# Gate and up products of the gated feed-forward parts by Strassen's scheme, in halves of 11 blocks

## The chip, the core and the metric

The kernel runs on one NeuronCore of a Trainium2 chip. Five engines work side by side, each through its own instruction queue in order: TensorE (PE, matrix products into PSUM), VectorE (DVE), ScalarE (ACT), GpSimd (POOL) and SyncE (SP, which issues DMAs). The metric is the device time of one execution in microseconds, as the median of several runs.

## What is computed

The reference is two transformer-like blocks over 512 tokens of width 1024. The first has two layers, each with a gated feed-forward part, a mixer of three kinds of heads, and a second gated feed-forward part. The second has a gated linear attention layer and a sparse attention layer, each followed by a convolutional feed-forward part. The change touches the four gated parts alone:

```python
def _swiglu(x, w_gate, w_up, w_down):
    return (jax.nn.silu(x @ w_gate) * (x @ w_up)) @ w_down

for l in range(DEPTH):                      # DEPTH = 2, D_FF = 2816
    x = x + 0.5 * _swiglu(_rms_norm(x, norm_ffn1[l]), ffn1_w_gate[l], ffn1_w_up[l], ffn1_w_down[l])
    ...                                     # mixer
    x = x + 0.5 * _swiglu(_rms_norm(x, norm_ffn2[l]), ffn2_w_gate[l], ffn2_w_up[l], ffn2_w_down[l])
```

All inputs are float32.

## The kernel before, in words

Activations lie feature-major: `x` is eight tiles of 128 features by 512 tokens. A float32 product is made of three reduced-precision (`float32r`) products: each operand is cut into a high part (ACT copies it into a `float32r` tile) and a low part (DVE subtracts the high part from the original), and PE accumulates hi x hi, hi x lo and lo x hi. `load_w` (L252) does this for a weight piece: a DMA on SP's queue into `raw`, ACT into `whi` (L258), DVE into `wlo` (L259). `raw` has three buffers, `whi` and `wlo` two each. `gemm` (L262) then issues three matmuls for each block of 128 inputs (L270 to L272), all with 512 tokens as columns.

A gated part is `ffn` (L361). `scaled` (L339) multiplies each `x` tile by the norm's gain and cuts it into `xh` and `xl`. `norm_r` (L321) computes the tokens' inverse norm R beside it: ACT squares, POOL adds the squares (L331), PE sums over partitions, and R comes as a tile `bR`. Then 22 blocks of 128 hidden features follow. Each has a gate product and an up product, of eight input blocks and three matmuls each (48 matmuls). DVE multiplies the gate product by R out of PSUM (L371), ACT applies silu (L372), POOL multiplies by R again (L373), DVE multiplies by the up product out of PSUM (L374), and `split` cuts the hidden block `h` (L287, L288). Afterwards `down` (L353) makes eight rows of output, each over all 22 hidden blocks in three weight pieces (66 matmuls), and DVE adds each to `x` (L359).

PSUM banks rotate through six names, so three blocks can be in flight. The order of instructions on each engine is set by a scheduler, from the order in which the code is written, priorities and a timeline of its own; buffers and semaphores hold whatever comes too early. The two convolutional parts (`conv_ffn`) have the same products and another elementwise chain; the change leaves their code as it is.

## Time and profile before

| | us |
|---|---|
| median of 3 runs | 3472.16 (3469.72 to 3480.32) |
| profiled execution, its own time | 3467.64 |
| its span, first to last instruction | 3464.6 |
| PE busy | 3419.1 (99%) |
| DVE busy | 1748.7 (50%) |
| ACT busy | 1232.1 (36%) |
| POOL busy | 538.8 (16%) |
| mean granted PE clock | 0.996 |

The span is what the trace covers; the profiled execution's own time has 3.0 us more around it. A row of the trace names the line of the kernel, the engine, the operation and the tiles (out<-in), and gives durations; an interval of idle time before an instruction stands in brackets with what ended it. The end of a matmul is modelled, and matmuls overlap: what one costs in a stream is the distance between two starts.

### The profile page before, as it was taken

The numbers are of one execution on the slowest core, as the hardware profiler recorded it, in microseconds if no ns is written. First come the engines' busy times: TensorE is split into PE (matmuls) and PEld (weight loads), VectorE is DVE, ScalarE is ACT, GpSimd is POOL, SyncE is SP. The second block draws the span as 40 slices with busy tenths as digits, with TensorE's granted clock in tenths as the row PEclk, the third lists the DMA queues.
The fourth block names the chain that finished last, engine by engine and source line by source line (L and its number), as shares of the span: only waits on it lengthen the run. The fifth ranks groups of instructions, "written<-read, shape, count | busy, mean of one in ns | idle before, by whom it ended". The sixth has DMA issues, their size and how long they took to land.

```text
span 3464.6 us, 43276 instructions
## 1 busy us (share of the span) xinstructions
PE 3419.1 (99%) x17126; PEld 2729.0 (79%) x17126; DVE 1748.7 (50%) x2857; ACT 1232.1 (36%) x1946; POOL 538.8 (16%) x509
## 2 busy tenths in 40 slices
PE   8999999999999999999999999999999999999998
PEld 6888777878888888877778888777888887778886
DVE  5333498663333433359765333385655354465532
ACT  3222334442222322233444222343433244643332
POOL 2110025011111111012401110020211000211100
PEclk9999999999999999999999999999999999999999
DMA  4223322132233223322123223322322333132232
GB/s 138 94 92 109 101 85 64 40 126 95 94 91 98 91 97 93 109 94 78 54 96 106 94 95 103 110 68 70 107 92 96 106 121 97 49 98 94 97 91 80
DMA packets 127593, 321.55 MB, mean 93 GB/s; under 512 B 32384, under 2 KB 34976, under 8 KB 127392
## 3 DMA queue, kind: packets, MB, share of 16 engines
q1 hardware_dynamic: 127392, 318.80, 29.0%
q8 instruction: 134, 2.20, 0.3%
q14 instruction: 67, 0.55, 0.0%
HBM read 303.81 MB, written 14.94 MB: 92 GB/s over the span
## 4 chain that ended last, share of the span: by engine, by line
PE 94%; DVE 3%; POOL 1%; DMA 1%; issue 1%; ACT 0%; SPq 0%; DVEq 0%; POOLq 0%; ACTq 0%
PE mm L272 13%; PE mm L270 13%; PE mm L271 13%; PE at L271 8%; PE at L270 8%; PE at L272 8%; PE rr L272 4%; PE rr L271 4%; PE rr L270 4%; PE rx L272 3%; PE rx L270 3%; PE rx L271 3%; PE po L749 1%; PE at L799 1%; PE at L743 1%
## 5 line engine op out<-in xcount | busy, mean ns | idle before, releaser
L258 ACT ACTIVATE whi<-raw 128x1024 fp32r<-128x1024 f32 (+2 forms) x566 | 562.6, 995 | 1685.2 <-issue 528.8
L259 DVE TENSOR_TENSOR wlo<-raw,whi 128x1024 fp32r<-128x1024 f32 (+2 forms) x566 | 650.7, 1150 | 502.0 <-ACT whi L258 486.2
L270 PE MATMUL mm<-xh,whi 128*128 128x512 f32 x1216 | 485.1, 399 | 9.1 <-ACT whi L258 9.0
L272 PE MATMUL mm<-xh,wlo 128*128 128x512 f32 x1216 | 487.5, 401 | 0.0
L271 PE MATMUL mm<-xl,whi 128*128 128x512 f32 x1216 | 484.7, 399 | 0.8 <-DVE xl L347 0.7
L272 PE MATMUL at<-xh,wlo 128*128 128x512 f32 x736 | 291.3, 396 | 0.0
L270 PE MATMUL at<-xh,whi 128*128 128x512 f32 x736 | 291.1, 395 | 0.0
L271 PE MATMUL at<-xl,whi 128*128 128x512 f32 x736 | 291.0, 395 | 0.0
L373 POOL TENSOR_TENSOR fg<-fg,bR 128x512 f32<-128x512 f32 x88 | 155.2, 1765 | 806.6 <-ACT fg L372 806.6
L270 PEld LDWEIGHTS mm<-xh,whi 128*128 128x128 f32 x1216 | 228.9, 188 | 65.1 <-ACT whi L258 9.5
L272 PEld LDWEIGHTS mm<-xh,wlo 128*128 128x128 f32 x1216 | 228.7, 188 | 60.6 <-issue 3.9
L271 PEld LDWEIGHTS mm<-xl,whi 128*128 128x128 f32 x1216 | 228.7, 188 | 57.3 <-issue 2.5
L270 PE MATMUL mm<-hi,whi 128*128 128x512 f32 x652 | 259.8, 400 | 3.3 <-ACT hi L287 1.5
L271 PE MATMUL mm<-lo,whi 128*128 128x512 f32 x652 | 258.2, 396 | 0.1
L272 PE MATMUL mm<-hi,wlo 128*128 128x512 f32 x652 | 257.5, 396 | 0.0
L331 POOL TENSOR_TENSOR nacc<-nacc,nsq 128x512 f32<-128x512 f32 x70 | 107.0, 1529 | 781.3 <-ACT nsq L330 780.8
L272 PEld LDWEIGHTS at<-xh,wlo 128*128 128x128 f32 x736 | 138.1, 188 | 35.5 <-DVE wl L514 1.5
L271 PEld LDWEIGHTS at<-xl,whi 128*128 128x128 f32 x736 | 138.2, 188 | 34.8 <-issue 1.5
L272 PE MATMUL rr<-xh,wlo 128*128 128x512 f32 x416 | 164.8, 396 | 0.8 <-DVE wlo L259 0.8
L270 PEld LDWEIGHTS at<-xh,whi 128*128 128x128 f32 x736 | 138.2, 188 | 34.1 <-ACT gy L1005 0.8
L271 PE MATMUL rr<-xl,whi 128*128 128x512 f32 x416 | 164.3, 395 | 0.0
L270 PE MATMUL rr<-xh,whi 128*128 128x512 f32 x416 | 164.2, 395 | 0.0
(667 smaller groups left out, 5878.8 us busy)
## 6 DMA issues: line engine op xcount, KB each, us to landing
raw<-ffn_gu SPq DMA_DIRECT2D x176, 512.0 KB
raw<-c_gu SPq DMA_DIRECT2D x88, 512.0 KB
raw<-ffn_dn SPq DMA_DIRECT2D x64, 448.0 KB
raw<-w_in SPq DMA_DIRECT2D x46, 512.0 KB
raw<-ffn_dn SPq DMA_DIRECT2D x32, 512.0 KB
raw<-c_dn SPq DMA_DIRECT2D x32, 448.0 KB
raw<-a_w_in SPq DMA_DIRECT2D x17, 512.0 KB
park<-x SPq DMA_DIRECT2D x32, 256.0 KB
```

Source lines behind the costliest of these rows:

```text
L258: self.A.activation(hi, raw, AF.Copy)
L259: self.V.tensor_tensor(lo, raw, hi.bitcast(F32), OP.subtract)
L270: self.T.matmul(ps, wh, xh, start=first and j == 0, stop=False)
L271: self.T.matmul(ps, wh, xl, start=False, stop=False)
L272: self.T.matmul(ps, wl, xh, start=False, stop=last and j == nk - 1)
L331: self.G.tensor_tensor(acc, acc, sq, OP.add)
L373: self.G.tensor_tensor(g, g, R, OP.mult)
L743: self.T.transpose(pt[:, b * 128:(b + 1) * 128], P[h][:, b * 128:(b + 1) * 128], self.ident)
L749: self.T.matmul(po[64 * h:64 * h + 64, i * 128:(i + 1) * 128], V(h, b), PT[h][:, b * 128:(b + 1) * 128], start=b == 0, stop=b == i)
L799: self.T.matmul(ps, q[b, i * 128:(i + 1) * 128], k[b, 0:(i + 1) * 128], start=True, stop=True)
```

## The change

For each block of 128 hidden features, gate and up together are a product of a 2 x 1024 block of weights with 1024 x 512 activations. The change splits the inputs into two halves of 512 features (p and q) and the tokens into two halves of 256 (a and b), and so has the 2 x 2 by 2 x 2 form on which Strassen's scheme (in Winograd's form) needs seven products in place of eight. Each product is over four blocks of 128 inputs, with three matmuls each and 256 columns.

`seven_x` takes the place of `scaled`. It forms the seven combinations of activations once for a part, and cuts each into hi and lo. `gate_up` takes the place of the two `proj` calls: POOL forms three sums and differences of the raw weight halves (s1, s2, and two written back into `ru` and `rg`), the weights are cut as G, S, U (each a `whi`/`wlo` pair of 1024 elements) and W (512), PE makes products 1 to 7 into two PSUM banks X and Y, and ACT and DVE combine them into gate and up. R for the up product moves from the block's chain into the addition of the output. The 22 blocks are worked in two halves of 11, each followed by a down product over its 11 hidden blocks (two weight pieces a row) that is added to `x`, on POOL after the first half and on DVE after the second. `raw` gets four buffers and `whi`/`wlo` three. At the start of the kernel two raw weight pieces are loaded early in place of two cut ones.

```diff
+HALF = ["r1"] * 8 + ["aq"] * 3
...
+    def raw(self, dram, cols):
+        raw = self.wp.tile([128, cols], F32, tag="raw", name=self.nm("raw"), bufs=4)
+        self.S.dma_start(raw, dram)
+        return raw
+
+    def parts(self, cols):
+        return [self.wp.tile([128, cols], F32R, tag=tag, name=self.nm(tag), bufs=3) for tag in ("whi", "wlo")]
...
+    def cut(self, src, hi, lo):
+        self.A.activation(hi, src, AF.Copy)
+        self.V.tensor_tensor(lo, src, hi.bitcast(F32), OP.subtract)
+
+    def seven_x(self, x, gname, l0):
...
+        for j in range(4):
+            scale(j)
+            self.V.tensor_tensor(xg[j][:, b], xg[j][:, b], xg[j][:, a], OP.subtract)
+            hi, lo = pair(self.other)
+            self.cut(xg[j], hi, lo)
...
+        for j in range(4):
+            scale(4 + j)
...
+            self.V.tensor_tensor(c[:, a], y[:, b], xg[j][:, b], OP.subtract)
+            self.V.tensor_tensor(c[:, b], y[:, a], c[:, a], OP.subtract)
+            hi, lo = pair(self.home)
+            self.cut(c, hi, lo)
...
+            self.cut(y, hi, lo)
...
+            self.V.tensor_tensor(d[:, e], c[:, a], xg[j][:, a], OP.subtract)
+            self.cut(d[:, e], dh[:, e], dl[:, e])
...
+    def gate_up(self, wgu, f, F, R):
...
+        s1, s2 = [self.s([128, H], "ws", heap="r0") for _ in range(2)]
+        S, G, U = self.parts(D), self.parts(D), self.parts(D)
+        self.G.tensor_tensor(s1, ru[:, p], ru[:, q], OP.add)
+        self.G.tensor_tensor(s2, s1, rg[:, p], OP.subtract)
+        self.cut(rg, *G)
+        self.cut(s2, *[t[:, q] for t in S])
+        self.cut(s1, *[t[:, p] for t in S])
+        self.G.tensor_tensor(ru[:, p], rg[:, p], ru[:, p], OP.subtract)
+        self.cut(ru, *U)
+        self.G.tensor_tensor(rg[:, q], rg[:, q], s2, OP.subtract)
...
+        self.cut(rg[:, q], *W)
...
+        A = {1: half(G, p), 2: half(G, q), 3: W, 4: half(U, q), 5: half(S, p), 6: half(S, q), 7: half(U, p)}
...
+                self.T.matmul(ps, hi[:, w], xh, start=first and j == 0, stop=False, skip_group_check=True)
+                self.T.matmul(ps, hi[:, w], xl, start=False, stop=False, skip_group_check=True)
+                self.T.matmul(ps, lo[:, w], xh, start=False, stop=j == 3, skip_group_check=True)
...
+        product(1, X[:, a], True)
+        self.A.activation(P[:, a], X[:, a], AF.Copy)
...
+                product(6, B, True)
+                self.V.tensor_tensor(v[:, a], B, P[:, a], OP.add)
...
+                product(5, X[:, b])
+                self.A.activation(P[:, b], X[:, b], AF.Copy)
+        product(4, E)
+        product(2, X[:, a])
+        self.V.tensor_tensor(g[:, a], X[:, a], R[:, a], OP.mult)
+        product(7, B)
+        self.V.tensor_tensor(v[:, b], B, P[:, a], OP.add)
+        self.V.tensor_tensor(u[:, a], E, v[:, b], OP.add)
+        self.V.tensor_tensor(u[:, b], v[:, b], P[:, b], OP.add)
+        product(3, X[:, b])
+        self.V.tensor_tensor(g[:, b], X[:, b], v[:, a], OP.add)
+        self.G.tensor_tensor(g[:, b], g[:, b], R[:, b], OP.mult)
+        self.A.activation(g, g, AF.Silu)
+        self.V.tensor_tensor(g, u, g, OP.mult)
+        return g
...
     def ffn(self, x, l, nm, wgu, wdn):
         self.on("o", "rr")
-        xs = self.scaled(x, nm, KT * l)
+        F = self.seven_x(x, nm, KT * l)
         R = self.norm_r(x)
...
-        for f in range(NF):
...
-        self.down(x, h.__getitem__, wdn, 0.5)
+        for part in range(2):
+            h = [self.split(self.gate_up(wgu, part * NF // 2 + i, F, R), None, HALF[i]) for i in range(NF // 2)]
+            for n in range(KT):
+                pd = self.ps([128, T], next(self.banks))
+                for a, b in ((0, 6), (6, 11)):
+                    o = part * NF // 2
+                    w = self.load_w(wdn[n, :, (o + a) * 128:(o + b) * 128], (b - a) * 128)
+                    self.gemm(pd, w, h.__getitem__, a, b, a == 0, b == NF // 2)
+                y = self.s([128, T], "fd")
+                self.V.scalar_tensor_tensor(y, pd, 0.5, R, OP.mult, OP.mult)
+                (self.V if part else self.G).tensor_tensor(x[n], x[n], y, OP.add)
```

In the words of the prediction, v_a and v_b, u_a and u_b, g_a and g_b are the halves of the tiles `fv`, `fu` and `fg` over tokens a and b; h hi and h lo are the cut hidden block.

On DVE, in the middle of a gate and up stage, this stands in the queue before, for one block and the start of the next (`lo` is the hidden block, `fg` the gate):

```order
L288 TENSOR_TENSOR lo_105_615<-fg_103_609,hi_104_614 128x512
L371 TENSOR_TENSOR fg_114_680<-mm_109_624,bR_45_202 128x512
L259 TENSOR_TENSOR wlo_119_692<-raw_117_689,whi_118_691 128x1024
L374 TENSOR_TENSOR fg_114_680<-rr_113_655,fg_114_680 128x512
L259 TENSOR_TENSOR wlo_123_723<-raw_121_720,whi_122_722 128x1024
L288 TENSOR_TENSOR lo_116_686<-fg_114_680,hi_115_685 128x512
```

and this after, at the same place in the first part, from the low part of the next block's G to that block's U:

```order
L373 TENSOR_TENSOR wlo_497_3053<-raw_490_3044,whi_496_3052 128x1024
L463 TENSOR_TENSOR fg_485_2942<-mm_482_2939,bR_67_260 128x256
L472 TENSOR_TENSOR fg_465_2809<-fu_466_2810,fg_465_2809 128x512
L465 TENSOR_TENSOR fv_487_2944<-rr_483_2940,wp_484_2941 128x256
L297 TENSOR_TENSOR lo_469_2908<-fg_465_2809,hi_468_2907 128x512
L466 TENSOR_TENSOR fu_486_2943<-rr_483_2940,fv_487_2944 128x256
L467 TENSOR_TENSOR fu_486_2943<-fv_487_2944,wp_484_2941 128x256
L373 TENSOR_TENSOR wlo_495_3051<-ws_492_3048,whi_494_3050 128x512
L469 TENSOR_TENSOR fg_485_2942<-mm_482_2939,fv_487_2944 128x256
L373 TENSOR_TENSOR wlo_495_3051<-ws_493_3049,whi_494_3050 128x512
L373 TENSOR_TENSOR wlo_499_3055<-raw_491_3046,whi_498_3054 128x1024
```

Between two blocks' G stand now thirteen operations (the eleven shown, and two more: v_a and W), where five stood for a block; the G of the next block comes before the last products of this one.

On POOL, behind the seven additions of squares at the start of the first part, this stands before:

```order
L331 TENSOR_TENSOR nacc_31_152<-nacc_31_152,nsq_37_169 128x512
L331 TENSOR_TENSOR nacc_31_152<-nacc_31_152,nsq_38_172 128x512
L373 TENSOR_TENSOR fg_48_254<-fg_48_254,bR_45_202 128x512
L373 TENSOR_TENSOR fg_59_325<-fg_59_325,bR_45_202 128x512
```

and this after (`ws` are s1 and s2 of block 0, `raw` its weights):

```order
L340 TENSOR_TENSOR nacc_53_210<-nacc_53_210,nsq_59_227 128x512
L340 TENSOR_TENSOR nacc_53_210<-nacc_53_210,nsq_60_230 128x512
L427 TENSOR_TENSOR ws_68_262<-raw_10_89 128x512
L428 TENSOR_TENSOR ws_69_263<-ws_68_262,raw_9_84 128x512
L432 TENSOR_TENSOR raw_10_89<-raw_9_84,raw_10_89 128x512
L434 TENSOR_TENSOR raw_9_84<-raw_9_84,ws_69_263 128x512
```

Where POOL went from the norm to one multiplication a block, it now forms block 0's weights behind the norm, and later repeats four such operations and one multiplication of 256 elements for every block:

```order
L427 TENSOR_TENSOR ws_492_3048<-raw_491_3046 128x512
L428 TENSOR_TENSOR ws_493_3049<-ws_492_3048,raw_490_3044 128x512
L432 TENSOR_TENSOR raw_491_3046<-raw_490_3044,raw_491_3046 128x512
L434 TENSOR_TENSOR raw_490_3044<-raw_490_3044,ws_493_3049 128x512
L470 TENSOR_TENSOR fg_485_2942<-fg_485_2942,bR_67_260 128x256
```

## Rows read from the trace of the kernel before

**Rows 1.** The page: span, and busy time of each engine.
```profile
span 3464.6 us, 43276 instructions
PE 3419.1 (99%) x17126; PEld 2729.0 (79%) x17126; DVE 1748.7 (50%) x2857; ACT 1232.1 (36%) x1946; POOL 538.8 (16%) x509
```
**Rows 2.** Busy time by stretch: 18 gate/up blocks, the kernel's start, one PE wait.
```profile
core 0: us, PE busy (x) PEld busy (x) DVE busy (x) ACT busy (x) POOL busy (x), PEclk, DMA share, GB/s
48.70:250.30 201.60, 201.60 (x866) 162.18 (x865) 79.83 (x90) 57.60 (x73) 32.60 (x18) 1.00 0.29 95
9.00:48.70 39.70, 38.02 (x158) 28.94 (x159) 26.53 (x34) 19.48 (x28) 16.52 (x10) 1.00 0.42 149
2394.00:2402.00 8.00, 6.43 (x20) 4.52 (x19) 3.65 (x6) 2.27 (x4) 0.00 (x0) 0.79 0.31 97
```
**Rows 3.** Timeline (start us, duration us) of DVE: two outputs of a down product.
```profile
276.86 0.69 DVE L359 SCALAR_TENSOR_TENSOR x<-at,x 128x512 f32<-128x512 f32 x1 [2.82 <-PE at L272]
292.26 0.69 DVE L359 SCALAR_TENSOR_TENSOR x<-mm,x 128x512 f32<-128x512 f32 x1 [2.82 <-PE mm L272]
```
**Rows 4.** Timeline of PE: first and last of 23 matmuls of 256 columns.
```profile
1795.33 0.28 PE L271 MATMUL mm<-ml,whi 128*128 128x256 f32 x1
...
1797.97 0.28 PE L272 MATMUL mm<-mh,wlo 128*128 128x256 f32 x1
```
**Rows 5.** Groups of DVE, same 18 blocks: count, then busy us, mean ns, idle before.
```profile
L259 DVE TENSOR_TENSOR wlo<-raw,whi 128x1024 fp32r<-128x1024 f32 x36 | 44.1, 1226 | 6.5 <-ACT whi L258 3.9
L288 DVE TENSOR_TENSOR lo<-fg,hi 128x512 fp32r<-128x512 f32 x18 | 12.3, 684 | 0.0
L374 DVE TENSOR_TENSOR fg<-at,fg 128x512 f32<-128x512 f32 x6 | 4.2, 692 | 19.9 <-PE at L272 19.9
```
**Rows 6.** Groups of POOL: those 18 blocks, convolutional parts, an operation of 256 elements.
```profile
L373 POOL TENSOR_TENSOR fg<-fg,bR 128x512 f32<-128x512 f32 x18 | 32.6, 1811 | 167.7 <-ACT fg L372 167.7
L396 POOL TENSOR_TENSOR cz<-cz,bR 128x512 f32<-128x512 f32 x44 | 56.8, 1291 | 431.0 <-ACT cz L395 431.0
L1226 POOL TENSOR_TENSOR cs<-cs,cok 128x256 f32<-128x256 f32 x4 | 2.9, 732 | 2.1 <-ACT cs L1225 2.1
```
**Rows 7.** Groups of DVE (256 elements out of PSUM) and ACT, whole span.
```profile
L574 DVE TENSOR_TENSOR SA<-rz,cpack 128x256 f32<-128x256 f32 x8 | 3.3, 416 | 0.6 <-PE rz L572 0.6
L258 ACT ACTIVATE whi<-raw 128x1024 fp32r<-128x1024 f32 x406 | 430.8, 1061 | 1247.3 <-issue 395.6 <-PE mm L271 347.6 <-PE at L271 259.0
L287 ACT ACTIVATE hi<-fg 128x512 fp32r<-128x512 f32 x88 | 55.8, 634 | 6.7 <-DVE fg L374 6.6
L745 ACT ACTIVATE sm_pt<-at 128x256 f32<-128x256 f32 x20 | 7.3, 387 | 6.5 <-PE at L743 6.4
```
**Rows 8.** Timeline of DVE and POOL in a gate and up stage.
```profile
66.37 1.23 DVE L259 TENSOR_TENSOR wlo<-raw,whi 128x1024 fp32r<-128x1024 f32 x1 [0.21 <-ACT whi L258]
66.93 1.81 POOL L373 TENSOR_TENSOR fg<-fg,bR 128x512 f32<-128x512 f32 x1 [9.39 <-ACT fg L372]
```
**Rows 9.** Timeline of DVE: two rows of the kernel's start, one without POOL.
```profile
14.22 2.30 DVE L259 TENSOR_TENSOR wlo<-raw,whi 128x1024 fp32r<-128x1024 f32 x1
16.44 5.18 DVE L347 SCALAR_TENSOR_TENSOR xl<-x,vec,xh 128x512 fp32r<-128x512 f32 x3
...
2391.32 1.29 DVE L288 TENSOR_TENSOR lo<-mq,hi 128x512 fp32r<-128x512 f32 x2
```
**Rows 10.** One line's instructions: count, then minimum, median and maximum ns.
```profile
L347 DVE SCALAR_TENSOR_TENSOR xl<-x,vec,xh x88: 734/749/1826, 4.9 to 3082.2; 128x512 fp32r<-128x512 f32 x88
```
**Rows 11.** Timeline of POOL and DVE at the end of a mixer.
```profile
736.51 1.30 POOL L331 TENSOR_TENSOR nacc<-nacc,nsq 128x512 f32<-128x512 f32 x1 [1.52 <-ACT nsq L330]
737.20 0.69 DVE L407 TENSOR_TENSOR x<-mm,x 128x512 f32<-128x512 f32 x1 [0.56 <-PE mm L272]
...
740.00 0.69 DVE L407 TENSOR_TENSOR x<-mm,x 128x512 f32<-128x512 f32 x1 [0.56 <-PE mm L272]
```
**Rows 12.** Timeline of PE: the wait of the last stretch in rows 2.
```profile
2397.03 0.73 PE L270 MATMUL mm<-hi,whi 128*128 128x512 f32 x2 [1.50 <-ACT hi L287]
```

More of the change, by code (lines that the diff above doesn't have):

```diff
@@ L202, in __init__ @@
         self.on("o", "rr")
-        self.ahead = []
+        self.ahead, self.raws = [], []
         self.cpack = self.cp.tile([128, CONST.shape[1]], F32, name="cpack")
@@ L248, in ps @@
         return self.pp.tile(shape, F32, tag=bank, name=self.nm(bank), bufs=BANKS[bank])
+    def raw(self, dram, cols):
[4 more added lines that the diff above has]
+        return [self.wp.tile([128, cols], F32R, tag=tag, name=self.nm(tag), bufs=3) for tag in ("whi", "wlo")]
     def load_w(self, dram, cols):
-        raw = self.wp.tile([128, cols], F32, tag="raw", name=self.nm("raw"), bufs=3)
-        self.S.dma_start(raw, dram)
-        hi = self.wp.tile([128, cols], F32R, tag="whi", name=self.nm("whi"), bufs=2)
-        lo = self.wp.tile([128, cols], F32R, tag="wlo", name=self.nm("wlo"), bufs=2)
+        raw = self.raw(dram, cols)
+        hi, lo = self.parts(cols)
         self.A.activation(hi, raw, AF.Copy)
@@ new lines, in gate_up, with product @@
+    def gate_up(self, wgu, f, F, R):
+        n, H = T // 2, D // 2
+        a, b = slice(0, n), slice(n, T)
+        p, q = slice(0, H), slice(H, D)
+        rg, ru = self.raws.pop(0) if self.raws else [self.raw(wgu[f, :, i * D:(i + 1) * D], D) for i in range(2)]
+        s1, s2 = [self.s([128, H], "ws", heap="r0") for _ in range(2)]
[8 more added lines that the diff above has]
+        self.G.tensor_tensor(rg[:, q], rg[:, q], s2, OP.subtract)
+        W = [self.s([128, H], nm, F32R, "ap") for nm in ("wsh", "wsl")]
+        self.cut(rg[:, q], *W)
+        half = lambda t, c: [y[:, c] for y in t]
+        A = {1: half(G, p), 2: half(G, q), 3: W, 4: half(U, q), 5: half(S, p), 6: half(S, q), 7: half(U, p)}
+        X, Y = [self.ps([128, T], next(self.banks)) for _ in range(2)]
+        def product(i, ps, first=False):
+            hi, lo = A[i]
+            for j in range(4):
+                xh, xl = F[i][j]
+                w = slice(j * 128, (j + 1) * 128)
+                self.T.matmul(ps, hi[:, w], xh, start=first and j == 0, stop=False, skip_group_check=True)
+                self.T.matmul(ps, hi[:, w], xl, start=False, stop=False, skip_group_check=True)
+                self.T.matmul(ps, lo[:, w], xh, start=False, stop=j == 3, skip_group_check=True)
+        P, g, u, v = [self.s([128, T], nm, heap="r0") for nm in ("wp", "fg", "fu", "fv")]
+        B, E = Y[:, a], Y[:, b]
+        product(1, X[:, a], True)
+        self.A.activation(P[:, a], X[:, a], AF.Copy)
+        for i in (5, 6) if f == 0 else (6, 5):
+            if i == 6:
+                product(6, B, True)
+                self.V.tensor_tensor(v[:, a], B, P[:, a], OP.add)
+            else:
+                product(5, X[:, b])
[13 more added lines that the diff above has]
+        return g
@@ L1469, in program @@
         x = [net.s([128, T], "x", heap="x") for _ in range(KT)]
-        first = ins["ffn1_gu0"]
+        first, raws = ins["ffn1_gu0"], []
         for k in range(KT):
@@ L1475, in program @@
             if k in (0, 3):
-                net.ahead.append(net.load_w(first[0, :, D * (k > 0):D * (k > 0) + D], D))
+                raws.append(net.raw(first[0, :, D * (k > 0):D * (k > 0) + D], D))
+        net.raws.append(raws)
         net.S.dma_start(net.cpack, ins["c_pack"])
@@ L1497 @@
     arrays = {"x": feat(a["x"][0]), "vecs": v.array(), "c_pack": CONST, **pack_first(a), **pack_second(a)}
-    nc = _bacc.Bacc("TRN2", target_bir_lowering=False, num_devices=1)
+    nc = _bacc.Bacc("TRN2", target_bir_lowering=False, num_devices=1, dynamic_dma_scratch_size=2048)
     ins = {n: nc.dram_tensor(n, w.shape, F32, kind="ExternalInput").ap() for n, w in arrays.items()}
```

32 lines of the change are left out of this document (23 added, 9 removed).

## The prediction

> **What bounds the kernel now.** I read the page first: TensorE (PE) is busy 3419.1 of 3464.6 us, the vector engine (DVE) 1748.7, GpSimd (POOL) 538.8 [rows 1]. Then the busy time by stretch. Eighteen blocks of one gate and up stage last 201.60 us with PE busy for all of it: 11.20 us a block, 48 matmuls of 512 columns, 0.2333 us each [rows 2]. In the down products two outputs are 15.40 us apart [rows 3], which is 66 matmuls at 0.2333 without a gap. So the four gated parts take 4 x (22 x 11.20 + 8 x 15.40) = 1478 us and are PE's; DVE is busy there for 79.83 us of 201.60 and POOL for 32.60. A faster PE is worth its time only until one of these becomes the limit, so I price all three per block.
>
> **PE.** Seven products of 4 k-blocks with three matmuls each make 84 matmuls of 256 columns a block. That size stands in the trace, with the same three-term pattern and a new weight for each: 22 steps from 1795.33 to 1797.97 us, 0.120 us a step [rows 4]. 84 x 0.120 = 10.08 us against 11.20; over 88 blocks 98.6 us, if PE stayed the limit. (The columns fall to 7/8, 9.80 us; the shorter matmul gives part of that back.)
>
> **What DVE and POOL get.** Before, a block costs DVE two weight subtractions of 1.23 us, one of 0.68, and two products out of PSUM of 0.69; POOL has one multiplication [rows 5, 6]. After, by the code and the two order pieces above, DVE has the subtractions G and U (1024 elements, 1.23 each), s1, s2, W and the hidden block (0.68 each), the last product u x g (0.68), u_b (256 elements, 0.41), and five 256-element operations that read PSUM (0.41 each [rows 7]): 5.9 + 0.4 + 2.05 = 8.3 us. POOL has four 512-element operations, 1.29 us each when alone, and one of 256, about 0.7 [rows 6]: 5.9 us. ACT comes to two copies of 1.06, five operations of 0.63 and two of 0.39, 6.05 us [rows 7]. Each by itself fits into 10.08.
>
> **DVE and POOL do not run independently.** POOL's multiplication takes 1.29 us in the convolutional stage and 1.81 in the gated one [rows 6]. The timeline shows why: it starts at 66.93, inside a weight subtraction that runs from 66.37 to 67.60, and ends 1.14 us after that one, at 68.74 [rows 8]. The other way round, at the start of the kernel, where POOL adds squares without a pause, three DVE operations take 5.18 us, 1.73 each, and a subtraction 2.30; alone they take 0.75 and 1.23 [rows 5, 9, 10]. So a DVE operation with two SBUF operands and a POOL operation take turns, and a contended pair costs 1.73, where the two durations add to 2.04: some 0.15 at the head and tail of each hides. A DVE operation that reads PSUM is free of it: at 737.20 it takes 0.69 while POOL runs its 1.30 [rows 11].
>
> Of the new DVE work 6.3 us a block has two SBUF operands, and POOL has 5.9. Taking turns, they need 12.1 us by full durations, and about 10.2 us if every change of turn hides its head and tail. Both ends are above PE's 10.08; nothing of the gain is sure.
>
> The Trainium skill's page "SBUF — State Buffer", section "SBUF: two separate sides", says that the shared port pair is an exclusive lock, which the first to start keeps for the whole instruction while the other fully blocks. The trace agrees on who blocks whom, with 1.81 for 1.29 us; on the price it differs a little, 1.73 for a pair and not 2.04. By the page's whole instructions a block would be 12.1 us, and by the sum below (8 x 131.1 = 1049, +63 + 46) the kernel 3581 us.
>
> **Which value.** The parts of a block are not free to shift: S, G and U have one buffer set each (three whi/wlo buffers), so a loop closes over one block. From the first use of S lo to the end of product 2, 34 matmuls x 0.120 + 0.16 (a matmul lasts 0.28 [rows 4]) = 4.24 us; G hi on ACT 1.06; then on DVE in the order shown G lo 1.23, g_a 0.41, u x g 0.68, v_b 0.41, h lo 0.68, u_a 0.41, u_b 0.41, s1 lo 0.68 = 4.91, less 0.08 at each of seven seams (two of 0.68 take 1.29 [rows 9]) = 4.35. Sum 9.65: without POOL, PE would stay the limit. POOL's subtraction on rg waits for G lo and so always falls into this stretch, +1.14 (what it took after its turn came in rows 8); h lo waits for its hi on ACT, 0.63 behind u x g, of which v_b covers 0.33, and a seam, +0.4: **11.2**. POOL's subtraction on ru, two places ahead in its queue, either gets its turn before G lo or just ahead of it in the loop, +1.14: **12.3**. I see no row that decides between the two and take the middle, **11.8 us a block**; bounds 10.1 (turns never collide) and 14.1 (all of DVE and POOL in series).
>
> In a half of 11 blocks the first finds its weights ready (7 x 12 x 0.120 = 10.1 us), ten follow at 11.8: 8 x (118 + 10.1) = 1025 us against 88 x 11.2 = 986: **+39 us** (by 11.2 -9, by 12.3 +79).
>
> **Down products.** As many matmuls as before. Two weight pieces a row in place of three, and one more addition of 0.7 to 1.3 us, off DVE or POOL, in 33 x 0.2333 = 7.7 us: covered. A half's first rows need 30 matmuls (7 us) before the last hidden block, whose chain (0.41 + 0.7 + 0.63 + 0.68 + 0.63 + 0.68) is about 4 us: covered. For four more turns between gate and down I take **+4 us** (0 to 10).
>
> **Starts of the four parts.** seven_x puts on DVE, with two SBUF operands, 4 x (0.41 + 0.68) + 4 x (4 x 0.41 + 2 x 0.68) = 16.4 us, where `scaled` had 8 x 0.75 = 6.0; POOL's seven adds of 1.29 go on, and by the order piece block 0's s1 and s2 stand behind all seven. At the start of the kernel that and block 0's own cuts (4.5 DVE, 5.2 POOL) add to 35 us, less hidden heads and tails about 30, for one block; before, PE was busy for 38.02 of the first 39.70 us [rows 2], 3.4 blocks. About 18 us lost there. After a mixer the x come 2.80 us apart (737.20, 740.00 [rows 11]); each of the last four now asks for 3.0 + 0.69 + 0.68 of DVE and 1.29 of POOL, about 5.5 us: 4 x 2.7, 10 us lost, twice. After another gated part the x come 7.7 us apart and only the last counts: 4 us. **+42 us**, bounds 15 and 85.
>
> DMA moves the same bytes, 95 GB/s before [rows 2], over a longer time. The added raw and whi buffers deepen the prefetch elsewhere; PE idles 45 us in all, so that is worth 0 to 10 us; I take 0.
>
> **Sum.** 39 + 4 + 42 = +85 us on the profiled execution's 3467.64, 3552.6; the median of the runs is 4.5 us above that execution, so **3557 us**.
>
> **Rivals.**
> - *PE stays the limit* (faster). If ru and the u x g product slip into the time in which DVE reads PSUM (2.05 us a block), the loop keeps its 9.65 and a block is 10.1: 8 x 10 x 10.1 + 81 = 889, -97 + 46 = -51, **3421**. For it: DVE and POOL have PSUM reads and idle time to overlap. Against it: 10.2 us of turns in 10.08. It decides at 11.2 a block minus the starts, so at about 10.7. Chance 15%.
> - *Near tie.* One POOL turn a block, partly hidden, 10.9, and starts near their lower bound: 8 x 119.1 = 953, -33 + 4 + 25: **3468**. 10%.
> - *The clock falls too* (slower still). In the loop PE waits 1.3 to 2.4 us once a block, ahead of the S products. After a wait of 1.50 us that ended at 2397.03 the granted clock fell to the lower of its two levels (1.2 for 2.4 GHz) for part of the next stretch, 0.79 on average over 8 us [rows 2, 12], so 1.7 us lost. Once a block that is 13.5: 8 x 145.1 = 1161, +175 + 46, **3693**. Against it: PE is busy for 10.08 us between two such waits. 5%.
> - The forecast, 11.2 to 12.6 a block with starts at 15 to 85: 70%.
>
> **How the numbers follow.** About 0.3%, 10 us, is what a measurement of this kernel can tell from no change. Faster 0.16 (the first rival and the low edge of the second), same 0.09, slower 0.75. The range 3450 to 3650 leaves out most of the first rival (0.12) and the clock case (0.06).
>
> **What would show it.** Right: POOL's new operations well above 1.29 us; two-operand subtractions above 1.23 and 0.68; PE waiting for `wlo` and `whi` inside the gate and up stage, a block every 11.2 to 12.3 us, while a step from matmul to matmul is 0.120 us. Wrong: blocks at 10.1 with PE always busy (the turns hide), steps longer than 0.120 (the size is mispriced), a granted clock well below 1 there (the clock), or a gap of more than 30 us at a start.

## The result, and the profile after

The changed kernel takes 3563.17 us (median of 4 runs, 3560.18 to 3567.92); the kernel before took 3472.66 us beside it. The ratio is 1.0264, 95% interval 1.0251 to 1.0277: slower by about 91 us. The profiled execution took 3560.40 us, with a span of 3558.6; against [rows 1] the span is 94.0 us longer.

The page of the changed kernel, span and busy time:

```profile
span 3558.6 us, 51753 instructions
PE 3372.3 (95%) x20294; PEld 2847.5 (80%) x20294; DVE 2391.6 (67%) x3753; ACT 1465.9 (41%) x2482; POOL 1187.8 (33%) x893
```

PE is busy 47 us less than in [rows 1] and the span is 94 us longer: 141 us of PE idle time came in. Where it lies is read from the busy time by stretch. A boundary is the end of DVE's last read of a half's down products, or the last addition of a mixer. Changed kernel, in order of time (first half and second half of the first part, first mixer, first halves of the second and third parts, second mixer, first half of the fourth part, linear attention):

```profile
core 0: us, PE busy (x) PEld busy (x) DVE busy (x) ACT busy (x) POOL busy (x), PEclk, DMA share, GB/s
0.00:226.40 226.40, 185.49 (x1208) 168.36 (x1209) 171.35 (x223) 96.43 (x155) 121.87 (x77) 1.00 0.32 103
226.40:409.30 182.90, 174.70 (x1186) 160.64 (x1185) 140.07 (x179) 76.69 (x121) 90.35 (x52) 1.00 0.35 108
409.30:780.50 371.20, 363.59 (x2479) 285.07 (x2477) 277.09 (x592) 158.68 (x306) 90.76 (x132) 0.98 0.25 75
780.50:985.20 204.70, 181.38 (x1196) 166.42 (x1197) 153.45 (x197) 80.62 (x130) 113.49 (x68) 0.95 0.29 88
1168.20:1375.60 207.40, 183.29 (x1203) 167.67 (x1202) 151.72 (x191) 80.96 (x130) 119.01 (x72) 0.95 0.27 86
1558.60:1926.70 368.10, 362.31 (x2479) 284.85 (x2477) 277.51 (x592) 159.02 (x306) 91.91 (x132) 0.99 0.26 76
1926.70:2129.30 202.60, 179.45 (x1196) 164.72 (x1197) 153.24 (x197) 80.81 (x130) 114.91 (x68) 0.96 0.28 88
2312.30:2539.40 227.10, 215.01 (x1113) 168.83 (x1113) 151.88 (x264) 102.25 (x178) 49.44 (x37) 0.98 0.24 77
```

The kernel before, for comparison (first part, first mixer, third part, linear attention; the second mixer lasts 362.10 there):

```profile
0.00:385.40 385.40, 374.72 (x1601) 299.80 (x1602) 150.91 (x178) 117.91 (x148) 60.46 (x39) 1.00 0.34 109
385.40:749.10 363.70, 356.84 (x2471) 283.43 (x2470) 271.74 (x580) 151.62 (x291) 83.65 (x126) 0.99 0.26 78
1120.00:1490.90 370.90, 370.90 (x1597) 298.60 (x1597) 137.81 (x164) 104.85 (x130) 49.96 (x29) 1.00 0.31 99
2223.90:2444.20 220.30, 215.77 (x1114) 169.55 (x1113) 147.21 (x263) 97.88 (x171) 39.01 (x31) 0.99 0.24 79
```

In steady state half a part took 11 x 11.2 + 8 x 7.7 = 184.8 us before. After, a second half takes 182.9 to 183.0: **1.8 us less, eight times, -14**. The rest of a first half is its start. After, the four first halves are 226.4 + 204.7 + 207.4 + 202.6 = 841.1 us, 109 more than four second halves; before, the four starts took 385.4 + 3 x 370.9 - 8 x 184.8 = 20. **Starts: +89.** The two mixers are 7.5 and 6.0 us longer, the linear attention 6.8: **+20**. All the rest is -1.

A steady stretch of eight blocks in a second half, first the busy times, then groups of DVE and POOL (count, busy us, mean ns, idle before), changed kernel:

```profile
255.30:344.90 89.60, 82.42 (x671) 80.69 (x671) 83.63 (x108) 44.19 (x74) 66.09 (x38) 1.00 0.28 88
...
L373 DVE TENSOR_TENSOR wlo<-raw,whi 128x1024 fp32r<-128x1024 f32 x15 | 30.2, 2014 | 0.0
L472 DVE TENSOR_TENSOR fg<-fu,fg 128x512 f32<-128x512 f32 x9 | 12.2, 1356 | 0.0
L297 DVE TENSOR_TENSOR lo<-fg,hi 128x512 fp32r<-128x512 f32 x9 | 8.7, 971 | 2.9 <-ACT hi L296 2.9
L373 DVE TENSOR_TENSOR wsl<-raw,wsh 128x512 fp32r<-128x512 f32 x8 | 7.6, 946 | 0.0
...
L432 POOL TENSOR_TENSOR raw<-raw,raw 128x512 f32<-128x512 f32 x8 | 18.2, 2269 | 0.0
L434 POOL TENSOR_TENSOR raw<-raw,ws 128x512 f32<-128x512 f32 x8 | 14.0, 1745 | 0.0
```

A block is 89.60 / 8 = 11.2 us, as long as before, though it has only 84 x 0.120 = 10.08 us of matmuls: PE waits 0.9 us once a block, for a `wlo` (S lo). POOL's operations of 512 elements take 1.62 to 2.27 us where one alone takes 1.29 [rows 6], G lo and U lo 2.01 where one takes 1.23 [rows 5], u x g (L472) 1.36 where an operation of its size takes 0.68 [rows 5]. DVE is busy 83.63 of 89.60.

The timeline shows the turns (start us, us; DVE first, then POOL):

```profile
308.83 2.31 DVE L373 TENSOR_TENSOR wlo<-raw,whi 128x1024 fp32r<-128x1024 f32 x1
311.06 0.41 DVE L463 TENSOR_TENSOR fg<-at,bR 128x256 f32<-128x256 f32 x1
311.40 1.44 DVE L472 TENSOR_TENSOR fg<-fu,fg 128x512 f32<-128x512 f32 x1
...
308.43 1.62 POOL L428 TENSOR_TENSOR ws<-ws,raw 128x512 f32<-128x512 f32 x1
310.00 2.29 POOL L432 TENSOR_TENSOR raw<-raw,raw 128x512 f32<-128x512 f32 x1
312.24 1.75 POOL L434 TENSOR_TENSOR raw<-raw,ws 128x512 f32<-128x512 f32 x1
```

G lo starts at 308.83 with POOL's s2 under way and lasts 2.31; POOL's next, on `ru`, waits for it in turn, and u x g for that one. Between the two DVE operations stands one that reads PSUM, 0.41 us, untouched.

At a start the same thing happens without a gap. Timelines at the second mixer's end, of DVE, POOL and PE (the wait before an instruction in brackets), and the granted clock there:

```profile
1928.33 1.48 DVE L400 TENSOR_TENSOR xc<-xg,xc 128x256 f32<-128x256 f32 x1
1931.14 1.75 DVE L373 TENSOR_TENSOR xl<-xc,xh 128x512 fp32r<-128x512 f32 x1
...
1928.12 1.41 POOL L340 TENSOR_TENSOR nacc<-nacc,nsq 128x512 f32<-128x512 f32 x1 [0.60 <-ACT nsq L339]
1929.48 1.45 POOL L427 TENSOR_TENSOR ws<-raw 128x512 f32<-128x512 f32 x1
...
1941.83 0.58 PE L448 MATMUL mm<-xh,wlo 128*128 128x256 f32 x1 [8.01 <-DVE wlo L373]
1942.21 0.42 PE L446 MATMUL mm<-xh,whi 128*128 128x256 f32 x1
1942.43 0.42 PE L447 MATMUL mm<-xl,whi 128*128 128x256 f32 x1
...
1930.70:1947.70 17.00, 6.67 (x29) 6.37 (x30) 16.45 (x29) 6.01 (x11) 9.03 (x7) 0.50 0.11 40
```

DVE and POOL alternate, one operation each: the 256-element operations, 0.41 us by themselves, take 1.48. PE waits 2.94 us up to 1929.58, 2.40 up to 1933.03 and then 8.01 for block 0's S lo. From 1930.70 on the granted clock stands at the lower level (0.50, 1.2 for 2.4 GHz) for 17.0 us, the last 5.9 of them with PE at work again. A step is 0.22 us there, not 0.120: the 6.67 us of PE work in that stretch would have taken about half.

### The profile page after: what moved, and what is told of

It reads as the page before. It is cut to its first block, busy times and chain, and to the rows that moved or that the text cites. A ratio compares the mean times of both kernels' runs of the same rounds, so it can differ in the third digit from the quotient of the medians.

```text
span 3558.6 us, 51753 instructions
## 1 busy us (share of the span) xinstructions
PE 3372.3 (95%) x20294; PEld 2847.5 (80%) x20294; DVE 2391.6 (67%) x3753; ACT 1465.9 (41%) x2482; POOL 1187.8 (33%) x893
## 4 chain that ended last, share of the span: by engine, by line
PE 43%; DVE 7%; issue 1%; ACT 1%; POOL 0%; DVEq 0%; ACTq 0%; POOLq 0%
PE mm L279 5%; PE mm L281 5%; PE mm L280 5%; PE at L279 3%; PE at L281 3%; PE at L280 3%; DVE wlo L373 2%; PE rx L281 1%; PE rx L279 1%; PE rx L280 1%; PE rr L281 1%; PE rr L279 1%; PE rr L280 1%; PE po L864 1%; DVE lo L297 1%
## 5 line engine op out<-in xcount | busy, mean ns | idle before, releaser
L267 ACT ACTIVATE whi<-raw 128x1024 fp32r<-128x1024 f32 (+4 forms) x422 | 380.8, 905 | 872.9 <-PE mm L280 356.7
L268 DVE TENSOR_TENSOR wlo<-raw,whi 128x1024 fp32r<-128x1024 f32 (+4 forms) x422 | 449.8, 1067 | 255.4 <-ACT whi L267 249.5
L373 DVE TENSOR_TENSOR wlo<-raw,whi 128x1024 fp32r<-128x1024 f32 x176 | 348.5, 1980 | 11.8 <-ACT whi L372 11.3
L281 PE MATMUL mm<-xh,wlo 128*128 128x512 f32 x736 | 296.7, 403 | 0.0
L448 PE MATMUL mm<-xh,wlo 128*128 128x256 f32 x768 | 222.9, 290 | 43.0 <-DVE wlo L373 42.9
L446 PE MATMUL mm<-xh,whi 128*128 128x256 f32 x768 | 221.0, 288 | 32.9 <-ACT wp L453 20.2
L447 PE MATMUL mm<-xl,whi 128*128 128x256 f32 x768 | 219.8, 286 | 4.5 <-DVE xl L373 4.5
L448 PE MATMUL at<-xh,wlo 128*128 128x256 f32 x672 | 193.2, 288 | 24.4 <-DVE wlo L373 24.4
L432 POOL TENSOR_TENSOR raw<-raw,raw 128x512 f32<-128x512 f32 x88 | 191.6, 2177 | 0.0
L446 PE MATMUL at<-xh,whi 128*128 128x256 f32 x672 | 190.5, 284 | 0.5 <-ACT wp L453 0.5
```

What stands on the lines that cost most here:

```text
L267: self.A.activation(hi, raw, AF.Copy)
L268: self.V.tensor_tensor(lo, raw, hi.bitcast(F32), OP.subtract)
L281: self.T.matmul(ps, wl, xh, start=False, stop=last and j == nk - 1)
L373: self.V.tensor_tensor(lo, src, hi.bitcast(F32), OP.subtract)
L432: self.G.tensor_tensor(ru[:, p], rg[:, p], ru[:, p], OP.subtract)
L446: self.T.matmul(ps, hi[:, w], xh, start=first and j == 0, stop=False, skip_group_check=True)
```

## The experiments

Each ratio is to runs of the kernel before on the same chip, whose medians lie between 3469.63 and 3472.92 us.

| run | what it is | median us | ratio to before, 95% interval |
|---|---|---|---|
| e1_narrow | weight sums cut down | 3438.65 | 0.9903, 0.9887 to 0.9920 |
| f1_psum | u x g through PSUM | 3474.48 | 1.0010, 1.0001 to 1.0020 |
| e6_both_dve | two weight sums to DVE | 3679.18 | 1.060, 1.058 to 1.062 |
| e3_norm_pe | norm's sum on PE | 3549.65 | 1.0225, 1.0205 to 1.0245 |
| s1_plain_x | no combinations of x | 3555.42 | 1.0245, 1.0230 to 1.0261 |
| d1_narrow2 | sums of two blocks a part cut down | 3517.38 | 1.0134, 1.0116 to 1.0152 |
| f2_start | f1 with less at the starts | 3466.56 | 0.9982, 0.9969 to 0.9995 |
| f3_prep | f1, block 0's weights first | 3497.37 | 1.0073, 1.0057 to 1.0089 |
| f4_prep_start | f2, block 0's weights first | 3473.36 | 1.0003, 0.9994 to 1.0012 |
| e4_halves | halves without Strassen | 3481.82 | 1.0025, 1.0014 to 1.0036 |
| b1_buf | before with the new buffers | 3474.28 | 1.0009, 0.9995 to 1.0024 |
| f5_plain2 | f1, two blocks a part plain | 3437.63 | 0.9904, 0.9887 to 0.9920 |

### The block: who is the limit

Theory: DVE's queue with the turns that POOL takes in it. Rival: the latency from DVE over PE and ACT back to DVE, whatever POOL does.

**e1_narrow.**

```diff
-        self.G.tensor_tensor(s1, ru[:, p], ru[:, q], OP.add)
+        self.G.tensor_tensor(ru[:, t], ru[:, t], ru[:, m], OP.add)
...
-        self.G.tensor_tensor(rg[:, q], rg[:, q], s2, OP.subtract)
+        self.G.tensor_tensor(rg[:, t], rg[:, t], ru[:, m], OP.subtract)
```

> POOL's four weight sums a block work on 32 of the 512 columns, in the same places and with the same dependences; most of each sum is left out, so S, G, U and W are cut from half-made weights. DVE, ACT and PE do as much as in the changed kernel. Theory (turns between POOL and the two-operand DVE subtractions make a block 11.2 us and lengthen the starts): the loop falls to its 9.65 without POOL, PE is the limit at about 10.1 us a block, a wlo subtraction of 1024 elements goes from a mean of 1.98 back to about 1.23 to 1.5 us; 80 blocks x 1.1 = 88 us less, and 5 to 10 us less at each start: 3563 falls to 3435 to 3475, at or below the kernel before. Rival (the loop is the latency from DVE to PE and ACT and would be 11.2 with POOL idle): a block stays at 11.2 and only the starts gain, 3535 to 3555.

The edit cuts all four of POOL's weight operations in a block down (the description of the change says three, and names four). 3438.65 us, 125 less than the changed kernel, in the theory's range. Eight steady blocks, and the groups of G lo, U lo and u x g there:

```profile
221.90:302.70 80.80, 80.80 (x677) 80.80 (x676) 66.47 (x106) 44.84 (x72) 20.26 (x40) 1.00 0.31 104
...
L373 DVE TENSOR_TENSOR wlo<-raw,whi 128x1024 fp32r<-128x1024 f32 x17 | 20.8, 1221 | 6.0 <-ACT whi L372 6.0
L472 DVE TENSOR_TENSOR fg<-fu,fg 128x512 f32<-128x512 f32 x9 | 6.2, 687 | 0.0
```

10.1 us a block, PE busy without a gap, the subtractions back at 1.22. In the steady block POOL's four operations were the whole difference. One reservation: with other durations the scheduler put a few of DVE's small operations in another order.

**f1_psum** has no such reservation: DVE's order in a block is that of the changed kernel, and all work is done.

```diff
-        self.A.activation(g, g, AF.Silu)
-        self.V.tensor_tensor(g, u, g, OP.mult)
-        return g
+        self.A.activation(X, g, AF.Silu)
+        self.V.tensor_tensor(Y, u, X, OP.mult)
+        return Y
```

> The changed kernel, with silu writing into bank X and u x g into bank Y, so that the product and the subtraction that cuts the hidden block read one operand from PSUM; nothing else moves, and DVE's order in a block stays. Theory (a DVE operation with two SBUF operands takes turns with POOL, one that reads PSUM does not; a block of 11.2 us is DVE's own queue with its turns): u x g falls from 1.30 to about 0.69 us, h lo from 0.97 to 0.68, about 1.07 us a block, so that a block comes to PE's 10.1: 8 steps in each of 8 halves x 1.1 = 70 us less, 3485 to 3505. Rival (POOL's operation then collides with the next two-operand subtraction, so the turn moves and is not saved): a block stays at 11.0 to 11.2, 3545 to 3563.

3474.48 us, 89 less than the changed kernel, more than the theory's 58 to 78 (its two terms add to 0.90 us a block, not 1.07; the block fell by 1.0). Eight steady blocks, a whole second half, and the groups of the first stretch:

```profile
235.20:316.80 81.60, 81.60 (x675) 81.03 (x674) 76.26 (x106) 43.17 (x72) 67.83 (x41) 1.00 0.32 103
217.50:391.10 173.60, 173.60 (x1188) 160.67 (x1187) 131.40 (x181) 76.78 (x121) 86.33 (x52) 1.00 0.37 113
...
L373 DVE TENSOR_TENSOR wlo<-raw,whi 128x1024 fp32r<-128x1024 f32 x16 | 32.6, 2035 | 0.0
L472 DVE TENSOR_TENSOR mm<-fu,at 128x512 f32<-128x512 f32 x3 | 2.0, 678 | 0.0
L297 DVE TENSOR_TENSOR lo<-rr,hi 128x512 fp32r<-128x512 f32 x3 | 2.1, 692 | 1.0 <-ACT hi L296 1.0
```

u x g costs 0.68 and h lo 0.69 with POOL as busy as before, G lo and U lo stay at 2.0: the turns taken away hardly come back elsewhere. PSUM by itself does not make u x g faster: in e1 it took 0.69 from SBUF. Every block is 10.2 us, and a half 173.6 for 183.0: 8 x 9.4 = 75 us; the remaining 14 lie in the starts and the mixers. The Trainium skill's page "SBUF — State Buffer", section "Who interferes with whom", says that a DVE instruction with at most one SBUF input, outside of the two-port performance modes, does not contend with GpSimd; this run agrees, 0.68 for 1.36 us.

**e6_both_dve.**

```diff
-        self.G.tensor_tensor(ru[:, p], rg[:, p], ru[:, p], OP.subtract)
+        self.V.tensor_tensor(ru[:, p], rg[:, p], ru[:, p], OP.subtract)
...
-        self.G.tensor_tensor(rg[:, q], rg[:, q], s2, OP.subtract)
+        self.V.tensor_tensor(rg[:, q], rg[:, q], s2, OP.subtract)
```

> The two subtractions of a block that make U and W from the raw halves (ru and rg) go from POOL to DVE; POOL keeps s1, s2 and one multiplication. Theory (in the loop DVE waits through a whole POOL operation for each turn, 1.14 us or more, and pays only 0.6 us for the same sum itself): the loop without POOL 9.65 grows by 0.6 to 1.2 us to 10.3 to 10.9, against 11.2: 80 x 0.3 to 0.9 = 24 to 72 us less, 3490 to 3540. Rival (DVE's own work is what counts): two more operations of 0.6 us make a block 11.8 to 12.4, 50 to 100 us more, 3610 to 3660.

3679.18 us, 116 more: the theory had the sign wrong, and the rival, 50 to 100 more and a block of 11.8 to 12.4 us, was too low. The timeline of DVE shows a second cause:

```profile
270.70:362.40 91.70, 75.98 (x589) 71.63 (x588) 80.09 (x106) 37.62 (x63) 30.87 (x21) 1.00 0.24 81
...
332.16 1.23 DVE L434 TENSOR_TENSOR raw<-raw,ws 128x512 f32<-128x512 f32 x1
333.32 1.76 DVE L373 TENSOR_TENSOR wlo<-ws,whi 128x512 fp32r<-128x512 f32 x1
...
342.08 0.43 DVE L465 TENSOR_TENSOR fv<-mm,wp 128x256 f32<-128x256 f32 x1 [1.17 <-PE mm L448]
```

A block is 91.70 / 7 = 13.1 us, 1.9 longer. DVE's own busy time is half of that (80.09 / 7 = 11.4 us a block for 83.63 / 8 = 10.5); the other half is more idle time on DVE (11.6 of 91.7 us for 6.0 of 89.6). The scheduler set the subtraction on `rg` between the two pieces of S lo, where it and the second piece of S lo now each wait for a turn of POOL (1.23 and 1.76 for 0.68). PE waits 1.1 us a block for exactly that piece, and DVE then waits 1.17 for PE. So the run prices a sum on DVE only together with this new order; that a turn in front of what PE waits for costs more than one elsewhere fits it, and was not tried by itself.

### The starts: +89 us

Candidates at a start: the norm's seven adds on POOL, the combinations of x on DVE, the weight sums of the first blocks on POOL.

**e3_norm_pe.**

```diff
-        R = self.norm_r(x)
+        R = self.norm_pe(x)
...
+                self.T.matmul(ss[:, j:j + 1], sq[:, j * 128:(j + 1) * 128], self.ones[:, 0:1], start=k == 0 and j == 0, stop=k == KT - 1,
+                              skip_group_check=True)
```

> In the gated parts the squares for the norm are summed over the k-blocks by PE (8 x 4 small matmuls into a bank) where POOL added them; the rest is the changed kernel. Theory (the starts lose some 82 us because POOL's seven adds stand ahead of block 0's sums and take turns with DVE's combinations): 7 turns of 1.3 to 1.8 us, 9 to 12 us of POOL, go at each of four starts; I expect 20 to 40 us less, 3523 to 3543, and the 256-element DVE operations there back from 1.48 to about 0.4 to 0.8 us for half of the stretch. Rival (the starts wait for DVE's own 16.4 us of combinations or for the x before them): no more than 10 us less, 3553 to 3563. The steady block stays at 11.2 either way.

3549.65 us, 13.5 less: for the whole kernel the theory was too high, the rival's "no more than 10" too low. The stretches say more. First mixer and the first half behind it:

```profile
406.50:783.90 377.40, 371.42 (x2535) 293.50 (x2534) 283.14 (x598) 161.01 (x309) 93.99 (x133) 0.98 0.24 74
783.90:976.70 192.80, 180.70 (x1196) 165.82 (x1197) 142.00 (x192) 79.09 (x127) 101.13 (x59) 0.97 0.29 93
```

The four first halves add up to 803.7 us for 841.1, so the starts are 37 us shorter, as the theory said. But the mixers ahead of two of them last 377.4 and 379.4 us for 371.2 and 368.1, with some 56 matmuls more in each: part of the gain is given back where PE now forms the sum.

**s1_plain_x.**

```diff
-            self.V.tensor_tensor(xg[j][:, b], xg[j][:, b], xg[j][:, a], OP.subtract)
...
-            self.V.tensor_tensor(c[:, a], y[:, b], xg[j][:, b], OP.subtract)
-            self.V.tensor_tensor(c[:, b], y[:, a], c[:, a], OP.subtract)
...
-            self.V.tensor_tensor(d[:, e], c[:, a], xg[j][:, a], OP.subtract)
```

> seven_x without its sums: the seven operands are cut from the scaled halves themselves (the subtractions on xg, xc and xd are left out; as many cuts and matmuls remain). Theory (the starts are long because DVE's combinations of x wait for POOL turn by turn): DVE's two-operand work at a start falls from 16.4 to about 9.8 us, by twice that where every operation waits for POOL, so 7 to 13 us less at each of four starts, 3510 to 3535. Rival (block 0 waits for its weight sums on POOL behind the norm's adds, the x are ready in time): less than 10 us in all, 3553 to 3563. A block stays at 11.2 either way.

3555.42 us, 8 less: the rival. The four first halves are 826.2 us, 15 less, and the two mixers 12 longer, for a reason that was not taken apart. So the combinations are a small part of the starts' 89 us, though they are the ones seen to take 1.48 us in the timeline. The cuts of x stay as they were in this run.

**d1_narrow2** has e1's edit for the first two blocks of a part and no other (the "40 first blocks' worth" in its text means nothing; the 89 us are those above).

```diff
+        if f < 2:
+            t, m = slice(0, 32), slice(H, H + 32)
+            s1, s2 = ru[:, p], rg[:, q]
+            self.G.tensor_tensor(ru[:, t], ru[:, t], ru[:, m], OP.add)
+            self.G.tensor_tensor(rg[:, m], ru[:, t], rg[:, m], OP.subtract)
```

> The changed kernel with the weight sums of the first two blocks of each part alone cut down to 32 of 512 columns; most of those sums is left out, all later blocks are as before. In the changed kernel the four starts cost some 89 us (40 first blocks' worth of waits and a lower clock); taking POOL's norm adds away gave 13 of it, taking DVE's combinations away 8. Theory (at a start POOL's two blocks of weight sums, 8 operations, share turns with DVE's x work and cuts): 25 to 40 us less, 3523 to 3538. Rival (the sums are not what the start waits for): 3553 to 3563.

3517.38 us, 46 less, more than the theory's 25 to 40. The first halves of the first three parts:

```profile
0.00:214.60 214.60, 182.77 (x1208) 167.64 (x1209) 159.56 (x223) 96.30 (x155) 114.78 (x77) 1.00 0.33 108
768.90:958.80 189.90, 177.97 (x1192) 163.91 (x1193) 142.19 (x195) 78.30 (x125) 102.17 (x60) 0.98 0.30 94
1141.80:1337.90 196.10, 181.04 (x1202) 166.45 (x1201) 143.47 (x187) 79.26 (x129) 111.71 (x66) 0.97 0.29 91
```

226.4, 204.7 and 207.4 have become 214.6, 189.9 and 196.1, the granted clock 0.95 has become 0.98 and 0.97; a second half stays at 183.0. The four first halves are 790.8 us, 50 less, so eight POOL operations a start are about half of the 89 us; some 9 of the 50 (8 x 1.1) any eight blocks would give.

Counted as above, the starts take 89 us in the changed kernel, 74 in s1, 52 in e3 and 39 in d1. None of the three candidates is the cause alone, and their gains of 15, 37 and 50 overlap, for together they are more than 89.

**f2_start** is f1_psum with e3's norm and with the scaled second half of x in PSUM.

```diff
-            xg[k] = self.s([128, T], "xg", heap="r0")
+            xg[k] = self.s([128, T], "xg", heap="r0") if k < 4 else self.ps([128, T], ("rr", "rx", "at", "at")[k - 4])
```

> f1_psum with the norm of the gated parts summed by PE, and with the scaled second half of x in PSUM, so that the subtractions that make c and cut y at a start read PSUM. If turns are the cause in the loop and at the starts alike: f1's 70 us, 13 us for the norm, and 3 x 0.68 + 2 x 0.41 of two-operand work less for each of four x at each of four starts, 2 to 8 us a start: 3450 to 3480, level with the kernel before or better. If only the loop follows the turns and the starts wait for the weights: 3475 to 3495.

3466.56 us, 8 less than f1: in the range of the first case only because f1 had already given 89 us and not 70. The four first halves are 769.0 us for f1's 796.8, 28 less, but the mixers are 14 us longer (368.9 and 376.3 for 365.7 and 365.2), with 56 matmuls more in each as in e3: half of the gain is lost ahead of the starts.

**f3_prep** and **f4_prep_start** write block 0's weight work ahead of the x work, on f1 and on f2.

```diff
+        A = {0: self.weights(wgu, 0)}
         F = self.seven_x(x, nm, KT * l)
```

> f1_psum with block 0's weight sums and cuts written ahead of seven_x, so that POOL has them among the norm's adds and not behind the last of them. If the starts wait for block 0's weights in POOL's queue: 2 to 8 us less at each start, 3445 to 3467 against f1's 3474. If POOL's whole work at a start is what counts, whatever its order (R then comes later instead): 3469 to 3479.

> f2_start with block 0's weight sums and cuts written ahead of seven_x; the norm is PE's there, so POOL has nothing else at a start. If the starts wait for block 0's weights: 2 to 8 us less at each start, 3435 to 3459 against f2's 3466.6, under the kernel before. If DVE's own x work and cuts are what is left: 3460 to 3470.

3497.37 and 3473.36 us, 23 more than f1 and 7 more than f2; neither case allowed for so much. The stretch ahead of a start shows where it went. f3, a second half that is followed by another gated part:

```profile
958.90:1137.90 179.00, 175.22 (x1200) 161.95 (x1198) 138.17 (x194) 81.32 (x132) 97.94 (x56) 1.00 0.30 95
```

179.0 us where f1 has 173.5, and both mixers are some 8 us longer than f1's, while the four first halves gain nothing (799.8 us for 796.8). So the weights prepared early made the work ahead of them longer and the starts no shorter. How that cost divides between POOL's turns and held buffers was not taken apart.

### The mixers and the linear attention: +20 us

**e4_halves.**

```diff
-            h = [self.split(self.gate_up(wgu, part * NF // 2 + i, F, R), None, HALF[i]) for i in range(NF // 2)]
+                pg = self.proj(wgu[f, :, 0:D], xs)
+                pu = self.proj(wgu[f, :, D:2 * D], xs)
...
+                h.append(self.split(g, None, HALF[i]))
```

> No Strassen: gate and up by the old projections of 48 matmuls of 512 columns, with the old scaling at the starts, but parts in halves of 11 blocks with two down products, R applied behind the down product, and the changed kernel's buffers (4 raw, 3 whi and wlo). It isolates halves and buffers. Theory (all of the 94 us comes from the seven products, at the starts and in what PE's thinner cover lets through): 3465 to 3485, the mixers and the linear attention as long as before, a block 11.2. Rival (the 20 us in the mixers and the linear attention come from the halves, from the x that are ready later or from the buffers): 3485 to 3500 with the mixers 6 to 8 us longer than before.

**b1_buf.**

```diff
-        raw = self.wp.tile([128, cols], F32, tag="raw", name=self.nm("raw"), bufs=3)
+        raw = self.wp.tile([128, cols], F32, tag="raw", name=self.nm("raw"), bufs=4)
```

> The kernel before with the changed kernel's buffers alone (4 raw, 3 whi and 3 wlo). The halves without Strassen cost 10 us, all of it in the two mixers and the linear attention. If the deeper prefetch of the weights is what costs there: 3478 to 3490. If the halves are (the last x of a part is added later, or the order of the norm's work differs): 3465 to 3475.

e4 takes 3481.82 us, 0.25% over before, just inside the theory's interval; but of its two cases the rival has the place right: its mixers last 369.5 and 369.3 us and its linear attention 227.6, as in the changed kernel. So that loss is not Strassen's alone. The buffers alone (with the DMA scratch setting that the change also made), 1.0009 with an interval that includes 1, explain at most a part. At the start of the linear attention the cause can be read. POOL's adds and PE's wait in the changed kernel; then the last add in the kernel before; then the adds in e4:

```profile
2313.62 11.14 POOL L340 TENSOR_TENSOR nacc<-nacc,nsq 128x512 f32<-128x512 f32 x7 [60.25 <-ACT nsq L339]
...
2334.17 1.09 PE L323 MATMUL po<-cpack,bex 128*128 128x128 f32 x4 [4.21 <-DVE bex L320]
```

```profile
2225.34 1.79 POOL L331 TENSOR_TENSOR nacc<-nacc,nsq 128x512 f32<-128x512 f32 x1 [13.86 <-ACT nsq L330]
```

```profile
2235.93 11.09 POOL L340 TENSOR_TENSOR nacc<-nacc,nsq 128x512 f32<-128x512 f32 x7 [184.72 <-ACT nsq L339]
```

Before, each square was added as its x came (POOL idle for 13.86 us ahead of the last, which takes 1.79); in halves ACT's squares come late and all seven adds follow the last x, 11.1 us. R comes later by most of that, and PE waits 4.21 us. This loss shows in every run with halves: the linear attention lasts 226.5 to 228.6 us in all of them, and 221.4 in b1, which has the buffers and no halves.

In the mixers PE hardly waits longer (371.20 - 363.59 = 7.6 us against 6.9), but its busy time is 363.59 for 356.84, with 8 matmuls more and a granted clock of 0.98 for 0.99: longer stretches at the lower level. That the halves set them off is not shown, for two mixers of the same code differ by as much in one execution: in e6, with halves, the first lasts 361.2 us at 1.00 and the second 371.5 at 0.97; in b1, without them, 373.7 at 0.97 and 362.8 at 0.99. So of the 20 us the 7 in the linear attention are explained, and the 13 in the mixers stay open.

### A version that beats both

**f5_plain2** is f1_psum with blocks 0 and 1 of each part computed without weight sums.

```diff
+            product(0, F[1], a, True)
+            self.A.activation(P[:, half], ps[:, a], AF.Copy)
+            product(0, F[5], b)
+            product(4, F[3], b)
+            product(4, F[2], a)
...
+    h = [self.split((self.plain if part * NF // 2 + i < 2 else self.gate_up)(wgu, part * NF // 2 + i, F, R), None, HALF[i]) for i in range(NF // 2)]
```

> f1_psum with the first two blocks of each part computed without weight sums: gate and up each from four products of x1a, x1b - x1a, x2a and x2b (8 products, 96 matmuls of 256 columns, 11.5 us a block against 10.1). POOL has only the norm's adds at a start and DVE only the cuts of gate and up. If POOL's first sums are what a start pays for (46 us for two blocks of four parts when they were cut down): about 46 less 8 x 1.4 = 35 us less than f1's 3474, so 3435 to 3450, faster than both kernels. If a start is held by the x work and the norm: 3465 to 3485.

3437.63 us, ratio 0.9904 (0.9887 to 0.9920), in the range of the first case: 35 us faster than the kernel before, 126 faster than the change, 37 faster than f1. First half of the third part:

```profile
1109.70:1290.40 180.70, 178.14 (x1226) 164.93 (x1225) 129.33 (x177) 76.55 (x125) 103.52 (x65) 1.00 0.29 94
```

PE's idle time in it is 2.6 us, where the changed kernel has 207.4 - 183.3 = 24.1 and f1 198.7 - 181.7 = 17.0, though two blocks have 12 matmuls more each. The four first halves are 756.5 us for f1's 796.8.

## Why the prediction came out as it did

The forecast was +85 us on the profiled execution, the measured change of the span +94. The direction and the mechanism (DVE and POOL take turns and become the limit) hold: e1 and f1 show it from both sides. The terms of the sum do not hold one by one. The halves and turn-overs came 57 us too high, the starts and the rest 66 too low; that 3557 lies 6 us from 3563.17 is luck.

- **PE, 10.08 us a block**: right. 84 steps of 0.120 us, and 10.1 to 10.2 us a block wherever PE doesn't wait.
- **The block, 11.8 us**: it is 11.2. The step that failed is "I see no row that decides between the two and take the middle": the lower of its two values was the block. The path was also another. The sum went from S lo over PE and ACT to G lo (4.24 + 1.06 us) and then through DVE. In the timeline DVE fills that time with U lo and W lo and their turns, and is busy 83.63 of 89.60 us: its whole queue is the loop, not a piece of it. By alone-durations (1.23 x 2, 0.68 x 5, 0.41 x 6) it needs 8.3 us; POOL's turns add 3.0 in a block (1.08 on G lo, 0.76 on u x g, 0.32 on h lo, 0.53 on U lo, 0.31 on W lo), seams take 0.8 off, waits add 0.7. (The upper bound, 14.1, is 14.2 by its own terms; nothing hangs on it.)
- **Halves, +39, and turn-overs, +4**: -14 together. With 11.2 the same formula gives -9.
- **Starts, +42**: 89, outside the bounds of 15 to 85. At the kernel's start and behind the two mixers 28, 20 and 18 us were lost, where the sum had 18, 10 and 10; behind another gated part 23, where it had 4, since it took only the last x to count there. In its place stand PE waits of 4.4 us for a copy of block 0's first product, 4.4 for S lo and 5.5 for R. The sum priced the weights at the kernel's start alone, and block 0's alone; d1 puts the sums of two blocks at four starts at 50 us. It left out that a short DVE operation waits for a whole operation of POOL (1.48 for 0.41), and the clock. Of the 109 us after, 40.9 + 23.3 + 24.1 + 23.2 - 4 x 8.2 = 79 are PE's waits; the other 30 are longer PE busy time, in part the lower clock (0.95 to 0.96 over three of the first halves; at the kernel's start steps of 0.21 us stand up to 42.9 us, though the view has 1.00 there). The x work and POOL's adds, which the sum did price, matter as well: s1 finds 15 us in the combinations, e3 37 in the adds.
- **Elsewhere, 0**: +20. The extra addition was called covered by the down products; what stands behind the last of them, the norm, was not looked at, and cost 7 us at the linear attention. The 13 us in the mixers are not explained.
- **Whole instructions in turn**, 12.1 us a block: the block is 11.2. The Trainium skill's page "SBUF — State Buffer", section "SBUF: two separate sides", has the shared port pair held for the whole instruction; the trace agrees that the two take turns, and has the lower price. The 6.3 us of two-operand DVE work and POOL's 5.9 stand in 11.2 us, so that at least 1.0 us of them overlaps.
- **Rivals.** PE did not stay the limit, but f1 shows how near it was: two operations that read PSUM in place of SBUF. The clock did not fall in the loop (1.00 in the steady stretch); it fell at the starts and in the mixers.
- **What would show it**: POOL's operations at 1.6 to 2.3 us, subtractions at 2.0, PE waiting for `wlo`, a block of 11.2 us with steps of 0.120 all came. No single gap of over 30 us came; the largest at a start are 11.47 us, at the kernel's own, and 8.01, behind a mixer.
